# Two weight sums of each Strassen unit move from GpSimd and SBUF to VectorE and PSUM, and some GpSimd operations get a wait on VectorE

## The chip, the cores and the metric

The kernel runs on one core of a Trainium2 chip. The metric is the device time of one execution in microseconds (us). Smaller is better. The engines are called PE (TensorE), DVE (VectorE), ACT (ScalarE), POOL (GpSimd) and SP (SyncE, which only issues transfers here).

## The reference

One decoder layer in float32 on 512 tokens of width 1024: a half-step SwiGLU feed-forward layer (FFN1, inner width 2816), a mixer (sliding-window attention, a causal depthwise convolution of 31 taps, two gates), a second half-step feed-forward layer (FFN2), and a gated embedding. What the change touches are the two feed-forward layers:

```python
def swiglu(h, w_gu, w_down):
    g, u = jnp.split(h @ w_gu, 2, axis=-1)
    return (jax.nn.silu(g) * u) @ w_down
...
        x = x + 0.5 * swiglu(rmsnorm(x, ffn1_norm[i]), ffn1_wgu[i], ffn1_wdown[i])
...
        x = x + 0.5 * swiglu(rmsnorm(x, ffn2_norm[i]), ffn2_wgu[i], ffn2_wdown[i])
```

## The kernel before

**Splitting.** Every float32 product is made of three matmuls in a rounded format: a weight or an activation v is split into hi = round(v), made by ACT, and lo = v - hi, made by DVE (`split_into`, line 701; a few of the lo are "flex", which means that the plan may give them to POOL). `mm3` then adds hi*hi, lo*hi and hi*lo. In the trace these are `whi_wgu`, `wlo_wgu` for the weights of gate and up, and `whi_wd`, `wlo_wd` for the weights of the down product.

**Units.** Most of a feed-forward layer is made of units (`unit`, line 947). A unit multiplies a weight of 2 x 2 blocks, A11, A12, A21, A22, with activations of 2 x 2 blocks by Strassen's way in Winograd's form: seven block products (f = 1 to 7) and some sums in place of eight products. Each of the seven weight forms is split by ACT and DVE, 1024 columns wide (768 in the last units of the down product). Four forms are sums of blocks. Two of them are made by the transfer itself: an accumulating DMA, issued by POOL, adds A22 onto A21, and later another one adds A21 onto A11. The two others are sums made by an engine, in two halves of 512 columns each: form 6 is A21 + A11 (after the first transfer), form 3 is A12 + form 6. They are called `wgu_s` and `wd_s` in the trace. They are flex, lie in SBUF, and POOL makes most of them.

There are 19 units for gate and up (`pair`, line 1062; two blocks of 128 inner columns each) and 12 for the down product (`down`, line 1095). A unit takes four PSUM banks; the running sums b1 and b2 in them are read by DVE and ACT between the products. In `down` DVE adds them onto the residual: operation `x<-wd_a,x` or `x<-wd_b,x`. PE can't go on accumulating in that bank before it is read. After a pair, `act_forms` (line 1046) makes the sums of activations that the down product needs (`f_ta`, `f_tb`, 128x256, flex) and splits them (`f_f`). `sums` (line 917) does the same for the normed input at the start of a layer (`f_xn`, `f_nh`, `f_nl`, `f_t`).

**What sets the order.** The program is recorded first, then a planner (`deadlines`, line 372, and `simulate`, line 404) plays it through with a cost for each operation and takes, on each engine, the ready operation that is due first. The order it finds is written out, and each engine then works through its own list strictly in that order, waiting where data or a buffer are not ready. One line issues everything (L1567), so instructions are told apart by their tiles. The planner knows that a DVE operation and a POOL operation can exclude each other: `op.lock` marks those it takes to be so, and it lets the second wait. Nothing in the emitted program enforces that order. Slots limit how far work runs ahead: 4 raw weight buffers, 4 hi, 4 lo, 8 PSUM banks (line 669). `DOWNS` (line 400) says after which pair the down products of which activations come; `deadlines` gives results in PSUM a due time after their group, 24 for the first plain products (marked `late`).

**The mixer** uses POOL for the convolution of three channel blocks (`y<-y,ct`, one add for each tap, line 1179), for lo splits, and for small work of the attention. At the end of an attention block DVE splits its result into `oT00l` and so on (`values`, line 1360, 128 columns each).

Of the kernel before, what the change touches and what calls it, by code (L numbers as in the profile page):

```python
# [16 lines left out]
P = 128  # L17
# [31 lines left out]
MARGIN = 0.0  # L49

CAPS = {"cz": 2, "ct": 4}
# [176 lines left out]
class Program:  # L228
# [69 lines left out]
    def costs(self, op, eng=None):  # L298
# [19 lines left out]
        elif eng == "DVE":  # L318
# [11 lines left out]
            op.lock = not psum and op.what not in ("tensor_tensor_reduce", "reduce_sum", "tensor_reduce", "reciprocal")  # L330
# [41 lines left out]
def deadlines(prog, when):  # L372
# [26 lines left out]
PLAIN, OWN = (4, 2), (False, False)  # L399
DOWNS = {10: [(0, 4)], 18: [(4, 8)], 20: [(8, 11)]}  # L400
# [3 lines left out]
def simulate(prog, slots):  # L404
# [39 lines left out]
    def can(op, slack):  # L444
# [6 lines left out]
        for v in op.writes:  # L451
            vt = v.vt
            if vt.slot is None:
                need.setdefault(vt.cls, {})[vt] = True
        for c, vts in need.items():
# [13 lines left out]
    def launch(op, t):  # L469
        nonlocal dma_free, aset, lock_dve, lock_pool  # L470
        for v in op.writes:
            vt = v.vt
            if vt.slot is None:
                vt.slot = free[vt.cls].popleft()
                if vt.kind:
                    inuse[vt.kind] += 1
# [195 lines left out]
def record():  # L672
# [274 lines left out]
    def unit(name, src, n, col, forms, own=False, first=None):  # L947
# [12 lines left out]
        sm = {f: [ftile(f"{name}_s{f}_{c}")[:, 0:half] for c in range(2)] for f in (6, 3)}  # L960
        for c in range(2):
            s = slice(c * half, (c + 1) * half)
            nc.flex.tensor_tensor(sm[6][c], A[21][:, s], A[11][:, s], op=ALU.add)
            nc.flex.tensor_tensor(sm[3][c], A[12][:, s], sm[6][c], op=ALU.add)

        def form(f):
            v = sm.get(f) or A[{1: 11, 2: 12, 5: 21, 7: 11, 4: 22}[f]]
            if f in sm and own:
                hi, lo = ([rtile(f"{name}_w{p}{f}_{c}")[:, 0:half] for c in range(2)] for p in "hl")
                for c in range(2):  # L970
                    split_into(hi[c], lo[c], v[c])
                return hi, lo
# [705 lines left out]
```

## Time and profile before

| | |
|---|---|
| median of 3 runs | 1189.03 us (1186.48 to 1191.82) |
| the profiled execution | 1190.71 us, its span 1189.0 us |
| PE, DVE, ACT, POOL busy | 1157.0, 1041.3, 698.0, 582.4 us |
| stages in the span | FFN1 0 to 350, mixer 350 to 800, FFN2 800 to 1150, last gate 1150 to 1189 |
| mean granted TensorE clock | 0.995 |

The span reaches from the first instruction to the last. The profiled execution takes 1.7 us beyond its span. A row of a group in the profile says what is written, what is read, the shape, how often, the busy time, the mean of one in ns, and how long the engine was idle just before such instructions and on whom it waited. Busy times on PE overlap, since matmuls are pipelined; what counts there is the idle time.

### The profile page before, as it was taken

The page shows a single profiled execution, that of the slowest core. Times are in us where ns is not written, and L with a number is a line of the kernel's source. Part 1 is how long each engine was busy: PE and PEld are TensorE (multiplying, and loading weights), DVE is VectorE, ACT ScalarE, POOL GpSimd, SP SyncE. Part 2 cuts the span into 40 slices and gives each one's busy share as a digit, 9 for nine tenths or more (in the row PEclk, how much of TensorE's full clock was granted, in tenths as well). Part 3 has the DMA queues.
Part 4 walks back from the last instruction along what each step waited for, and adds up shares of the span by engine and source line. Part 5 has one row for each costly group of instructions (what it writes and reads, how often), then busy time and mean ns, then how long its engine had stood idle before and what let it go on. Part 6 is the DMA issues. An engine that isn't in the chain of part 4 may idle for free. (4 is left out here: it accounts for less than half of the span.)

```text
span 1189.0 us, 19980 instructions
## 1 busy us (share of the span) xinstructions
PE 1157.0 (97%) x7532; PEld 1056.7 (89%) x7532; DVE 1041.3 (88%) x1582; ACT 698.0 (59%) x1248; POOL 582.4 (49%) x563
## 2 busy tenths in 40 slices
PE   9989999999999999989999999999999999999998
PEld 7889999999999887868788878889999999999986
DVE  6999999978996898999999975579888998798997
ACT  7556546654555679869964472446755456446642
POOL 1666354534425986888799300034663552237400
PEclk9999999999999999999999999999999999999999
DMA  7545657666534321311222323344765566545421
GB/s 242 143 124 143 177 143 170 158 160 158 140 88 123 105 72 43 100 53 37 89 89 93 121 88 95 100 107 109 193 161 160 127 176 156 153 119 139 126 89 71
DMA packets 46752, 146.88 MB, mean 124 GB/s; under 512 B 5696, under 2 KB 10432, under 8 KB 46656
## 3 DMA queue, kind: packets, MB, share of 16 engines
q1 hardware_dynamic: 37584, 114.12, 28.9%
q0 software_dynamic: 8928, 31.46, 15.9%
q8 instruction: 59, 0.97, 0.3%
q14 instruction: 37, 0.30, 0.1%
q10 hardware_dynamic: 144, 0.03, 0.0%
HBM read 143.50 MB, written 2.10 MB: 122 GB/s over the span
## 5 line engine op out<-in xcount | busy, mean ns | idle before, releaser
L1567 DVE TENSOR_TENSOR wlo_wgu<-raw_wgu,whi_wgu 128x1024 fp32r<-128x1024 f32 (+1 forms) x131 | 153.9, 1182 | 20.5 <-ACT whi_wgu L1567 20.2
L1567 ACT ACTIVATE whi_wgu<-raw_wgu 128x1024 fp32r<-128x1024 f32 (+1 forms) x131 | 116.2, 900 | 71.5 <-PE wgu_b L1567 26.4
L1567 PE MATMUL wgu_b<-f_t_h,wlo_wgu 128*128 128x256 f32 x456 | 130.6, 286 | 2.4 <-DVE f_gs L1567 1.8
L1567 PE MATMUL wgu_b<-f_t_l,whi_wgu 128*128 128x256 f32 x456 | 129.9, 285 | 1.5 <-DVE f_t_l L1567 1.5
L1567 PE MATMUL wgu_b<-f_t_h,whi_wgu 128*128 128x256 f32 x456 | 129.7, 284 | 0.0
L1567 POOL TENSOR_TENSOR y<-y,ct 128x509 f32<-128x509 f32 (+28 forms) x90 | 114.1, 1288 | 5.1 <-ACT ct L1567 3.8
L1567 ACT ACTIVATE whi_wd<-raw_wd 128x1024 fp32r<-128x1024 f32 (+1 forms) x60 | 59.3, 988 | 94.2 <-PE wd_b L1567 53.2
L1567 POOL DMA_DIRECT2D raw_wgu<-in_wgu x38 | 34.2, 915 | 162.4 <-DVE x L1567 98.5
L1567 DVE SCALAR_TENSOR_TENSOR cz<-u,dww,cz 128x486 f32<-128x486 f32 (+24 forms) x145 | 101.7, 729 | 1.1
L1567 PEld LDWEIGHTS wgu_b<-f_t_h,wlo_wgu 128*128 128x128 f32 x456 | 87.9, 193 | 3.4 <-ACT f_t_h L1567 2.0
L1567 PEld LDWEIGHTS wgu_b<-f_t_l,whi_wgu 128*128 128x128 f32 x456 | 87.9, 193 | 1.9 <-DVE f_t_l L1567 1.9
L1567 PEld LDWEIGHTS wgu_b<-f_t_h,whi_wgu 128*128 128x128 f32 x456 | 88.0, 193 | 0.0
L1567 PE MATMUL wgu_a<-f_nh,wlo_wgu 128*128 128x256 f32 x304 | 86.2, 284 | 1.1 <-DVE wlo_wgu L1567 1.1
L1567 PE MATMUL wgu_a<-f_nl,whi_wgu 128*128 128x256 f32 x304 | 86.3, 284 | 1.0 <-DVE f_nl L1567 1.0
L1567 PE MATMUL wgu_a<-f_nh,whi_wgu 128*128 128x256 f32 x304 | 86.0, 283 | 0.0
L1567 DVE TENSOR_TENSOR wlo_wd<-raw_wd,whi_wd 128x1024 fp32r<-128x1024 f32 (+1 forms) x60 | 74.2, 1237 | 7.5 <-ACT whi_wd L1567 7.1
L1567 PE MATMUL wd_a<-f_f_h,wlo_wd 128*128 128x256 f32 x264 | 75.3, 285 | 4.4 <-DVE x L1567 4.4
L1567 PE MATMUL wd_b<-f_f_h,wlo_wd 128*128 128x256 f32 x264 | 75.5, 286 | 2.5 <-DVE x L1567 2.0
L1567 PE MATMUL wd_a<-f_f_l,whi_wd 128*128 128x256 f32 x264 | 75.2, 285 | 0.5 <-DVE f_f_l L1567 0.5
L1567 PE MATMUL wd_b<-f_f_l,whi_wd 128*128 128x256 f32 x264 | 75.1, 284 | 0.0
L1567 PE MATMUL wd_b<-f_f_h,whi_wd 128*128 128x256 f32 x264 | 75.1, 284 | 0.0
L1567 PE MATMUL wd_a<-f_f_h,whi_wd 128*128 128x256 f32 x264 | 75.0, 284 | 0.0
(512 smaller groups left out, 4216.9 us busy)
## 6 DMA issues: line engine op xcount, KB each, us to landing
raw_wgu<-in_wgu SPq DMA_DIRECT2D x80, 512.0 KB, 4.4
raw_wgu<-in_wgu POOLq DMA_DIRECT2D x38, 512.0 KB, 5.6
raw_wd<-in_wd SPq DMA_DIRECT2D x32, 512.0 KB, 4.4
raw_wd<-in_wd POOLq DMA_DIRECT2D x16, 512.0 KB, 5.5
raw_wzc<-in_wzc SPq DMA_DIRECT2D x16, 512.0 KB, 3.6
raw_wzg<-in_wzg SPq DMA_DIRECT2D x16, 512.0 KB, 3.6
raw_wd<-in_wd SPq DMA_DIRECT2D x16, 384.0 KB, 3.4
raw_wgu<-in_wgu SPq DMA_DIRECT2D x32, 128.0 KB, 3.8
```

The lines of the kernel that those rows point to most:

```text
L1567: getattr(engines[op.eng], op.what)(*a, **k)
```

## The change

- `unit`: forms 6 and 3 are made by DVE alone (`nc.vector`), into two PSUM tiles, `zs`, one bank each. First z = A21 + A11. When form 6 is due, z is split (ACT reads z, DVE computes lo = z - hi), then z = A12 + z is made in place, and split as form 3. The four SBUF tiles of the sums are gone, and so is the unused option `own`.
- The planner takes both `zs` tiles of a unit together (`mate`), lets only one unit at a time have them (`CAPS`), and not earlier than 24 ahead of their due time (`LEADS`).
- `op.lock` now also holds for DVE operations with one operand in PSUM if two of their inputs lie in SBUF.
- The due time of `late` results is 8 in place of 24.
- `DOWNS`: the first down product follows pair 8 in place of pair 10; the second follows pair 20 in place of pair 18, next to the third.
- `turns` goes through the finished plan. Where the planner started a POOL operation later than its data, its buffer and POOL itself allowed, and a locking DVE operation ended in that time, the POOL operation gets a real wait on that DVE operation. The plan has 46 such waits, 28 of them on POOL's operations in the feed-forward layers.

```diff
-CAPS = {"cz": 2, "ct": 4}
+LATE = 8.0
+LEADS = {"zs": 24.0, "zt": 14.0}
+CAPS = {"cz": 2, "ct": 4, "zs": 2, "zt": 2}
...
-            op.lock = not psum and op.what not in ("tensor_tensor_reduce", "reduce_sum", "tensor_reduce", "reciprocal")
+            two = sum(v.vt.cls != "ps" and v.free() > 1 for v in ins) > 1
+            op.lock = two if psum else op.what not in ("tensor_tensor_reduce", "reduce_sum", "tensor_reduce", "reciprocal")
...
-                            ls = min(ls, gend[o.group] + (24.0 if v.vt.late else 5.0))
+                            ls = min(ls, gend[o.group] + (LATE if v.vt.late else 5.0))
...
-DOWNS = {10: [(0, 4)], 18: [(4, 8)], 20: [(8, 11)]}
+DOWNS = {8: [(0, 4)], 20: [(4, 8), (8, 11)]}
...
         half = n // 2
-        sm = {f: [ftile(f"{name}_s{f}_{c}")[:, 0:half] for c in range(2)] for f in (6, 3)}
-        for c in range(2):
-            s = slice(c * half, (c + 1) * half)
-            nc.flex.tensor_tensor(sm[6][c], A[21][:, s], A[11][:, s], op=ALU.add)
-            nc.flex.tensor_tensor(sm[3][c], A[12][:, s], sm[6][c], op=ALU.add)
+        done = {}
+        cuts = [slice(c * half, (c + 1) * half) for c in range(2)]
+        zs = [nc.tile(f"zs_{name}_{c}", [P, S], F32, "ps")[:, 0:half] for c in range(2)]
+        for z, s in zip(zs, cuts):
+            nc.vector.tensor_tensor(z, A[21][:, s], A[11][:, s], op=ALU.add)
...
+        def summed():
+            done[6], done[3] = pieces(6), pieces(3)
+            for z, s in zip(zs, cuts):
+                split_into(*(p[:, s] for p in done[6]), z)
+                nc.vector.tensor_tensor(z, A[12][:, s], z, op=ALU.add)
+                split_into(*(p[:, s] for p in done[3]), z)
...
+def turns(prog):
+    held, last, vec, free, busy = {}, {}, [], {}, 0.0
...
+        if op.eng == "DVE" and op.lock:
+            vec.append(op)
+        if op.eng == "POOL":
+            if op.lock and op.start > max(ready, busy) + 0.05:
+                for o in reversed(vec[-40:]):
+                    if o.start + o.cost <= op.start + 0.05:
+                        if o.start + o.cost > max(ready, busy):
+                            held[op] = o
+                        break
+            busy = op.start + op.cost
+    return held
...
-            getattr(engines[op.eng], op.what)(*a, **k)
+            made[op] = getattr(engines[op.eng], op.what)(*a, **k)
+            if op in held:
+                tc.add_manual_dep(made[op].ins, made[held[op]].ins.name, sync, reason="port")
```

PE issues the same matmuls as before, and in the mixer in the same order of groups; in the feed-forward layers the down units stand elsewhere. POOL loses 99 sums, DVE had made the other 25 of the 124 and now makes all.

**DVE at the start of FFN1, before.** These rows end the splits of the normed input (`f_nl`), make the activation sums `f_t`, and begin with form 6 of the first unit, whose sum `wgu_s` comes from POOL.

```order
L1567 TENSOR_TENSOR f_nl_640<-f_xn_526,f_nh_541 128x512 [waits DVE_49]
L1567 TENSOR_TENSOR f_nl_646<-f_xn_537,f_nh_551 128x512 [waits DVE_49]
L1567 SCALAR_TENSOR_TENSOR f_t_0_657<-f_t_0_486,f_xn_510 128x256
L1567 SCALAR_TENSOR_TENSOR f_t_0_657<-f_t_0_486,f_xn_517 128x256
L1567 SCALAR_TENSOR_TENSOR f_t_1_674<-f_t_1_504,f_xn_526 128x256
L1567 SCALAR_TENSOR_TENSOR f_t_1_674<-f_t_1_504,f_xn_537 128x256
L1567 TENSOR_TENSOR wlo_wgu_6_696<-wgu_s_0_531,whi_wgu_6_601 128x512 [waits Activation_49]
```

The same place on DVE after the change:

```order
L1611 TENSOR_TENSOR f_nl_653<-f_xn_544,f_nh_561 128x512 [waits Activation_49]
L1611 TENSOR_TENSOR f_nl_660<-f_xn_564,f_nh_580 128x512 [waits Activation_49]
L1611 TENSOR_TENSOR f_gs_669<-f_g_538,f_n_rb 128x512 [waits PE_49]
L1611 TENSOR_TENSOR zs_wgu_0_679<-raw_wgu_21_416,raw_wgu_11_385 128x512 [waits DMASW0_49]
L1611 TENSOR_TENSOR zs_wgu_1_687<-raw_wgu_21_416,raw_wgu_11_385 128x512
L1611 SCALAR_TENSOR_TENSOR f_t_0_696<-f_t_0_487,f_xn_523 128x256
L1611 SCALAR_TENSOR_TENSOR f_t_0_696<-f_t_0_487,f_xn_529 128x256
L1611 SCALAR_TENSOR_TENSOR f_t_1_709<-f_t_1_505,f_xn_544 128x256
L1611 TENSOR_TENSOR wlo_wgu_6_718<-zs_wgu_0_679,whi_wgu_6_698 128x512 [waits Activation_49]
```

The sums now stand in DVE's own list, ahead of `f_t`, and the first of them waits there for the accumulating transfer (`DMASW`).

**POOL in the mixer, before**, around two lists of convolution adds (y_5793 and y_5386 are channel blocks 4 and 2):

```order
L1567 TENSOR_TENSOR y_5793<-y_5793,ct_5_5947 128x507
L1567 TENSOR_TENSOR wlo_wzg_6182<-raw_wzg_5986,whi_wzg_6168 128x1024 [waits DMAHW5_49,PE_49,Activation_49]
L1567 TENSOR_TENSOR y_5793<-y_5793,ct_6_5970 128x506 [waits Pool_49]
L1567 TENSOR_TENSOR y_5386<-y_5386,ct_8_5991 128x504
L1567 TENSOR_TENSOR y_5793<-y_5793,ct_7_6134 128x505 [waits Pool_49]
L1567 TENSOR_TENSOR y_5386<-y_5386,ct_9_6192 128x503 [waits Activation_49,Pool_49]
L1567 TENSOR_TENSOR y_5793<-y_5793,ct_8_6221 128x504 [waits Activation_49,Pool_49]
L1567 TENSOR_TENSOR y_5386<-y_5386,ct_10_6236 128x502 [waits Activation_49,Pool_49]
```

The same place after the change (y_5773 and y_5355):

```order
L1611 TENSOR_TENSOR y_5773<-y_5773,ct_6_5934 128x506
L1611 TENSOR_TENSOR wlo_wzg_6148<-raw_wzg_5960,whi_wzg_6134 128x1024 [waits DMAHW5_49,PE_49,Activation_49]
L1611 TENSOR_TENSOR zq_3_5987<-zq_3_5987,qcs 128x8x16 [waits Pool_49]
L1611 TENSOR_TENSOR y_5355<-y_5355,ct_8_5943 128x504 [waits DVE_49]
L1611 TENSOR_TENSOR zq_3_5987<-zq_3_5987,q_3_w 128x8x16 [waits Pool_49]
L1611 TENSOR_TENSOR y_5773<-y_5773,ct_7_6066 128x505 [waits DVE_49]
L1611 TENSOR_TENSOR y_5355<-y_5355,ct_9_6074 128x503 [waits Pool_49]
L1611 TENSOR_TENSOR y_5773<-y_5773,ct_8_6160 128x504 [waits Activation_49,Pool_49]
```

Two of the adds now wait on DVE. The operations they wait for are `oT00l` and `oT01l` of the last token block, the first of which stands two rows behind the `oT00l` of the block before it in DVE's list.

More of the change, by code (lines that the diff above doesn't have):

```diff
@@ L66, in __init__ @@
         self.late = False
+        self.mate = None
         self.kind = name[:2] if name[:2] in CAPS else None
@@ L462, in can @@
                 return False
+            if slack > min(LEADS.get(vt.kind, 1e9) for vt in vts):
+                return False
             if len(free[c]) < len(vts) + spare:
                 return False
-            if any(vt.kind and inuse[vt.kind] >= CAPS[vt.kind] for vt in vts):
+            if any(vt.kind and inuse[vt.kind] + (vt.mate is not None) >= CAPS[vt.kind] for vt in vts):
                 return False
@@ L471, in launch @@
         for v in op.writes:
[L472 to L476, printed above, removed]
+            for vt in (v.vt, v.vt.mate):
+                if vt is not None and vt.slot is None:
+                    vt.slot = free[vt.cls].popleft()
+                    if vt.kind:
+                        inuse[vt.kind] += 1
         c = op.cost
@@ L945, in record, with unit @@
     lo_, hi_ = slice(0, HS), slice(HS, S)
-    def unit(name, src, n, col, forms, own=False, first=None):
+    def unit(name, src, n, col, forms, first=None):
         A = {}
@@ L988, in times @@
                     c = col(k, m)
-                    wk = part([p[c // half] for p in w], slice(c % half, c % half + P)) if isinstance(w[0], list) else part(w, slice(c, c + P))
+                    wk = part(w, slice(c, c + P))
                     mm3(to[m], wk, x_, start and k == 0, k == len(forms[f]) - 1, skip=f in (3, 4, 6, 7))
@@ L1003, in unit, with ffn @@
             yield 4, m, b1[m], b2[m]
-    def ffn(tag, wgu, wdown, h, gain, ss, after, cuts, wide, plain, own, mid=None):
+    def ffn(tag, wgu, wdown, h, gain, ss, after, cuts, wide, plain, mid=None):
         rb = None
@@ L1538, in record @@
     return nc
+def turns(prog):
+    held, last, vec, free, busy = {}, {}, [], {}, 0.0
+    for vt in prog.tiles:
+        vt.ops = []
+    for op in prog.ops:
+        for vt in op.vts:
+            vt.ops.append(op)
+    for op in sorted(prog.ops, key=lambda o: (o.start, o.i)):
+        ready = max((o.end for o in op.preds), default=0.0)
+        for vt in op.outs:
+            slot = vt.cls, vt.slot
+            was = last.get(slot)
+            if was is not vt:
+                free[slot] = max((o.end for o in was.ops), default=0.0) if was else 0.0
+                last[slot] = vt
+            if vt.ops[0] is op:
+                ready = max(ready, free[slot])
+        if op.eng == "DVE" and op.lock:
[9 more added lines that the diff above has]
+    return held
 def hybrid_layer(tc, aps):
@@ L1562, in real @@
             return v
+        made = {}
+        held = turns(prog)
+        sync = mybir.DependencyInfo(mybir.DependencyClass.Sync, mybir.DependencyReason.DATA)
         for op in sorted(prog.ops, key=lambda o: (o.start, o.i)):
```

35 lines of the change are left out of this document (15 added, 20 removed).

## The prediction

> **What bounds the kernel now.** I read the page first, then busy time by stage, then who waits for whom on PE, then the timeline at the largest waits.
>
> ```profile
> PE 1157.0 (97%) x7532; PEld 1056.7 (89%) x7532; DVE 1041.3 (88%) x1582; ACT 698.0 (59%) x1248; POOL 582.4 (49%) x563
> ```
>
> Busy time by stretches of the span (us, then for PE, weight loads, DVE, ACT and POOL the busy us and the number of instructions, the granted clock, the DMA share and GB/s). The first row is from the middle of FFN1, the others are FFN1, mixer and FFN2:
>
> ```profile
> 200.00:250.00 50.00, 50.00 (x419) 50.00 (x419) 45.99 (x60) 32.12 (x56) 23.99 (x19) 1.00 0.70 177
> ...
> 50.00:350.00 300.00, 291.33 (x2375) 288.72 (x2374) 273.10 (x376) 164.54 (x268) 142.66 (x117) 0.99 0.58 147
> 350.00:800.00 450.00, 440.24 (x2068) 364.55 (x2067) 379.72 (x621) 289.44 (x566) 263.91 (x292) 1.00 0.28 88
> 800.00:1150.00 350.00, 343.48 (x2732) 335.92 (x2731) 318.15 (x455) 202.12 (x331) 157.38 (x127) 1.00 0.55 144
> ```
>
> In the middle of FFN1 PE never stops: nothing can be won there, since the change leaves the matmuls as they are. What can be won is PE's idle time: 8.7 us in FFN1 (300 - 291.33), 9.8 in the mixer, 6.5 in FFN2. In both feed-forward layers DVE is the next fullest engine, with 26.9 and 31.9 us free.
>
> For what did PE wait? The largest entries (total us, times, longest): one from the whole span, then FFN1 (50 to 350), then FFN2 (800 to 1150):
>
> ```profile
> PE sc L1567 <- DVE sga L1567: 4.9, 1, 4.9
> ...
> PE wd_a L1567 <- DVE x L1567: 2.0, 1, 2.0
> PE wgu_b L1567 <- DVE f_gs L1567: 1.8, 1, 1.8
> PE wgu_b L1567 <- DVE f_t_l L1567: 1.5, 2, 1.2
> PE wgu_a L1567 <- DVE wlo_wgu L1567: 1.1, 2, 0.6
> PE wgu_a L1567 <- DVE f_nl L1567: 1.0, 1, 1.0
> ...
> PE wd_a L1567 <- DVE x L1567: 2.4, 2, 1.3
> PE wd_b L1567 <- DVE x L1567: 1.7, 1, 1.7
> PE wgu_a L1567 <- DVE f_t_l L1567: 1.1, 1, 1.1
> ```
>
> Always DVE, in few long pieces: 4.9, 7.4 and 5.2 us. Why was DVE late? The timeline at the largest wait (mixer) and at one in FFN2 (start, us, instruction):
>
> ```profile
> 513.80 7.70 DVE L1567 TENSOR_TENSOR oT00l<-of,oT00h 128x128 fp32r<-128x128 f32 x1
> 512.21 2.40 POOL L1567 TENSOR_TENSOR wlo_wzg<-raw_wzg,whi_wzg 128x1024 fp32r<-128x1024 f32 x1
> 514.57 6.78 POOL L1567 TENSOR_TENSOR y<-y,ct 128x506 f32<-128x506 f32 x6
> 522.75 0.75 PE L1567 MATMUL sc<-kzh,qT_l 128*128 128x512 f32 x1 [4.89 <-DVE sga L1567]
> ...
> 1058.83 3.02 DVE L1567 TENSOR_TENSOR wlo_wd<-wd_s,whi_wd 128x512 fp32r<-128x512 f32 x1
> 1058.91 1.71 POOL L1567 TENSOR_TENSOR f_tb<-f_us,f_us 128x256 f32<-128x256 f32 x2
> ```
>
> A DVE operation of 128 columns lasted 7.70 us: from inside one POOL instruction to the end of six more (514.57 + 6.78 = 521.35). Everything behind it on DVE stood, and PE with it. At 1058.83 it is the same on a smaller scale, and PE's wait of 1.7 us for `x` is the consequence. So an operation of DVE that reads SBUF twice is shut out while POOL works, and a POOL that never pauses shuts it out for its whole run. The Trainium skill ("SBUF — State Buffer", section "Who interferes with whom") says that of two such instructions the later blocks until the earlier instruction ends; by that rule `oT00l` would have gone on at 514.6, PE would have lost nothing here, and the sum below would lack its first term of 6.6 us. The trace disagrees: seven instructions passed.
>
> A long wait costs more than itself. Granted clock (third number from the end) right after the waits of 1.8, 2.0 and 4.9 us:
>
> ```profile
> 75.40:79.20 3.80, 3.61 (x17) 3.64 (x18) 3.80 (x8) 3.40 (x6) 0.71 (x1) 0.55 0.00 0
> 331.40:335.20 3.80, 3.80 (x21) 3.80 (x20) 2.85 (x6) 0.00 (x0) 0.67 (x1) 0.55 0.34 124
> 522.60:526.40 3.80, 3.65 (x11) 2.98 (x12) 3.04 (x11) 2.35 (x5) 0.00 (x0) 0.55 0.00 0
> ```
>
> 0.55 of full speed over 3.8 us loses 1.7 us each time. All in reach: 4.9 + 7.4 + 5.2 + 3 x 1.7 = 22.6 us.
>
> **The change part by part.** DVE's rows by shape (count, busy us, mean ns):
>
> ```profile
> L1567 DVE TENSOR_TENSOR wlo_wgu<-raw_wgu,whi_wgu 128x1024 fp32r<-128x1024 f32 x99 | 141.5, 1430 | 20.1 <-ACT whi_wgu L1567 19.9
> L1567 DVE TENSOR_TENSOR wlo_wgu<-wgu_s,whi_wgu 128x512 fp32r<-128x512 f32 x76 | 69.4, 942 | 0.5 <-ACT whi_wgu L1567 0.5
> L1567 DVE TENSOR_TENSOR wlo_wd<-wd_s,whi_wd 128x512 fp32r<-128x512 f32 x32 | 32.7, 1036 | 0.0
> L1567 DVE TENSOR_TENSOR p_l<-pT,p_h 128x512 fp32r<-128x512 f32 x16 | 10.2, 680 | 0.2
> L1567 DVE TENSOR_TENSOR wlo_wgate<-raw_wgate,whi_wgate 128x1024 fp32r<-128x1024 f32 x8 | 9.6, 1214 | 0.0
> L1567 DVE TENSOR_TENSOR pg_ss_acc<-pg_ss_acc,pg_ss_sq 128x512 f32<-128x512 f32 x5 | 3.5, 692 | 0.0
> L1567 DVE TENSOR_TENSOR pg_ss_acc<-pg_ss_sq,pg_ss_sq 128x512 f32<-128x512 f32 x1 | 0.7, 695 | 0.0
> ```
>
> *Sums added to DVE.* The last two rows are the new operations: two SBUF inputs into PSUM 0.695 us, PSUM plus SBUF in place 0.692. Of 124 sums, 108 have 512 columns: 108 x 0.69 = 74.5 us. The 16 of 384 columns cost between half and all of that; I take three quarters, 0.52: 8.3. DVE made 25 before, at least 25 x 0.69 = 17.3 of its time. Added: 65.5 us. The Trainium skill ("Advanced Engine Details and Errata", section "The Read-Write Bubble") places VectorE nearer to SBUF than to PSUM and advises using it so, which speaks against this move. Rows 692 and 695 against 680 agree in sign, but it is 0.015 us on each of 124, under 2 us of DVE.
>
> *Shut-out time taken off DVE.* `p_l` has the operands that the splits of the sums will have (PSUM and SBUF) and takes 0.680; the same splits from SBUF take 0.942 and 1.036. That is 76 x 0.262 + 32 x 0.356 = 31.3 us. The other splits keep both inputs in SBUF: 99 x (1.430 - 1.214) = 21.4 us shut out, measured against `wlo_wgate`, which runs while POOL is still. They gain as far as POOL has less to do:
>
> ```profile
> L1567 POOL TENSOR_TENSOR wgu_s<-raw_wgu,raw_wgu 128x512 f32<-128x512 f32 x29 | 50.7, 1763 | 39.3 <-DMA raw_wgu<-in_wgu 39.3
> L1567 POOL TENSOR_TENSOR wgu_s<-raw_wgu,wgu_s 128x512 f32<-128x512 f32 x28 | 48.1, 1725 | 11.1 <-DMA raw_wgu<-in_wgu 10.7
> L1567 POOL TENSOR_TENSOR wd_s<-raw_wd,wd_s 128x512 f32<-128x512 f32 x14 | 22.0, 1575 | 12.3 <-DVE f_us L1567 9.8 <-DMA raw_wd<-in_wd 1.8 <-DVE f_f_l L1567 0.7
> L1567 POOL TENSOR_TENSOR wd_s<-raw_wd,raw_wd 128x512 f32<-128x512 f32 x13 | 19.6, 1524 | 38.2 <-DMA raw_wd<-in_wd 31.3 <-DVE f_f_l L1567 6.9
> ```
>
> These alone are 140.4 of POOL's 142.7 + 157.4 = 300.1 us in the two layers, and they come in runs of two to four. With 47% less POOL, some 10 us of the 21.4 go. DVE's balance is then 65.5 - 31.3 - 10 = +24 us in 650, inside its 58.8 free. It stays nearly as full, but it is no longer stopped for several us at a time, and that is what PE felt.
>
> *Waits on PE that go.* In the mixer, the adds behind `wlo_wzg` now wait for `oT00l` and `oT01l`, so POOL pauses there; `oT00l` is held 2.4 us at most in place of 7.7, and PE's 4.9 has no cause left: -4.9 - 1.7 = -6.6 (ends -6.6 and 0). FFN1 loses 7.4 + 2 x 1.7 = 10.8. Two of its waits (`f_nl`, `f_t_l`) are on the crowded list at its start, where the new sums stand ahead of `f_t`; I take two thirds, -7 (ends -10.8 and 0). FFN2: two thirds of 5.2, -3.5 (ends -5.2 and 0), since `f_ta` and `f_tb`, the cause at 1058.9, stay on POOL.
>
> *New waits.* `DOWNS` puts four down units at the end of each layer, so the last pair's activation sums have the (4, 8) units to hide behind; its gain lies in the terms above. Inside a down unit PE needs each `x` operation before it accumulates on, and DVE's list now holds sums that wait for an accumulating transfer. `zs` takes 2 of 8 banks, 4 belong to the running unit, so the next unit starts with 2. For both together I take +2 us (below zero is excluded, as nothing waits less for them; the upper end is the slower rival). The 46 waits on POOL: behind one stand POOL's later operations and the accumulating transfers; POOL is idle for 350 of the 650 us, so zero. `LATE` and `LEADS` only shift due times: zero.
>
> Sum: -6.6 - 7 - 3.5 + 2 = -15.1. The profiled execution would take 1190.7 - 15.1 = 1175.6; it lies 1.7 above the median, so the median 1189.0 becomes 1173.9, say 1174.
>
> **The rivals.**
>
> *DVE keeps PE waiting all the same (0.20).* DVE stays at over 90% in both layers, and operations that come in order fall late without POOL's help. Then only the mixer's wait goes, and half of the rest comes back in new places with its clock: 1189 - 6.6 + 2 = 1184, between 1180 and 1189. For it: +24 us. Against it: in the rows 200 to 250 DVE was 46.0 of 50 with PE never waiting.
>
> *DVE stands at the transfers (0.13, slower).* POOL waited for accumulating transfers before it summed:
>
> ```profile
> POOL wgu_s L1567 <- DMA raw_wgu<-in_wgu: 49.9, 14, 6.9
> POOL wd_s L1567 <- DMA raw_wd<-in_wd: 40.0, 10, 7.2
> ```
>
> 24 waits, 89.9 us, 3.7 each. Now the sum stands in DVE's list and everything behind it waits too, the `x` operations above all. DVE has 58.8 - 24 = 35 us left to hide that. Beyond 35 it reaches PE, and from 35 + 15 = 50 us on the kernel is slower. With two thirds inherited (60 us): 1174 + 25 = 1199; with all, 1229. For it: the lists are strict, and the wait is in the order. Against it: POOL came early because it was free half the time, and the planner places a DVE sum by its due time.
>
> *The change doesn't do what it says (0.07).* POOL's waits don't open a gap where DVE needs it, or the runs of `f_ta`, `f_tb` and `y` shut DVE out in other places: 1189, give or take 5.
>
> **How the numbers follow.** The forecast case, 1165 to 1182, has 0.60. A difference under 0.5% (6 us) can't be told from none here, since the three runs spread over 5.3 us. Faster by more: 0.60, and half of the first rival: 0.70. Slower by more: 0.13 and a little of the last one, less what of the transfers' rival ends near zero: 0.12. Within: 0.18. The range starts where everything in reach goes (1189.0 - 22.6 = 1166, less 1 for the spread), 1165, and ends at 1191, which takes in the first rival and most of the last and leaves the transfers' rival out.
>
> **What would show it.** Right: no `oT` operation over 2.7 us on DVE; `wlo_wgu<-zs` at 0.68 and `zs` sums at 0.69 to 0.9 us; POOL busy near 160 us in the two layers; PE's waits under 8 us in all, and fewer drops of the clock. Wrong: entries of DVE waiting on `raw_wgu` or `raw_wd` transfers that sum to more than 35 us; PE's idle time in the layers at 15 us or more; a wait of PE for banks held by `zs`.

## The result, and the profile after

The changed kernel takes 1171.38 us (1170.37 to 1172.17, 4 runs), the kernel before 1190.42 in the same comparison: ratio 0.9844, 95% interval 0.9816 to 0.9872. It is faster by 19 us. The prediction said 1174 in a range from 1165 to 1191, so the number was right. The experiments show which parts of the working behind it hold.

Two corrections to the sections ahead of the prediction. No tile's `mate` is ever set, so the two `zs` tiles aren't taken as one; only `CAPS` holds them to two at a time. And FFN2 starts before 800: its first matmul stands at 782.0 in the kernel before and at 763.8 after the change.

The span is 1169.1 us. The page's busy times, to be held against PE 1157.0, DVE 1041.3 and POOL 582.4 of before:

```profile
PE 1152.4 (99%) x7532; PEld 1054.3 (90%) x7532; DVE 997.4 (85%) x1670; ACT 692.2 (59%) x1246; POOL 440.9 (38%) x475
```

Busy time in the stretches of the prediction (PE, weight loads, DVE, ACT, POOL, the granted clock). The last one ends at 1130, because FFN2 ends earlier:

```profile
50.00:350.00 300.00, 297.19 (x2453) 296.22 (x2452) 267.72 (x434) 167.50 (x274) 72.66 (x69) 0.99 0.61 152
350.00:800.00 450.00, 444.79 (x2090) 367.88 (x2090) 378.49 (x634) 293.59 (x579) 272.27 (x300) 1.00 0.29 89
800.00:1130.00 330.00, 327.71 (x2632) 321.67 (x2631) 284.25 (x472) 187.72 (x310) 78.54 (x77) 1.00 0.59 148
```

PE's idle time in them was 8.7, 9.8 and 6.5 us; now it is 2.8, 5.2 and 2.3. That is 14.7 us less. But the second stretch now holds the start of FFN2. Between the first and the last matmul of each stage PE idled 9.0, 9.8 and 6.2 us before, and idles 2.8, 2.6 and 3.9 now, 15.5 us less in all. Stretches of 1.9 us in which the clock was under 0.75 were six before, and there is one now; summed as (1 - clock) x 1.9 that is 4.8 us before and 1.0 after, another 3.8. Together that is roughly 19 of the span's 19.9 us. Whom PE waited for (total, times, longest; the wait for `ones` at the start of the program left out):

```profile
PE wgu_b L1611 <- DVE f_gs L1611: 3.3, 2, 1.8
PE gb L1611 <- DVE s L1611: 1.2, 1, 1.2
...
PE wgu_b L1611 <- ACT f_gs L1611: 1.1, 1, 1.1
```

The waits for `sc` (4.9) and for the `x` operations are gone, and no piece is longer than 1.8 us. DVE by shape (count, busy, mean ns, idle before):

```profile
L1611 DVE TENSOR_TENSOR wlo_wgu<-raw_wgu,whi_wgu 128x1024 fp32r<-128x1024 f32 x99 | 124.7, 1261 | 37.6 <-ACT whi_wgu L1611 37.5
L1611 DVE TENSOR_TENSOR wlo_wgu<-zs_wgu,whi_wgu 128x512 fp32r<-128x512 f32 x76 | 49.1, 679 | 4.9 <-ACT whi_wgu L1611 4.8
L1611 DVE TENSOR_TENSOR zs_wgu<-raw_wgu,zs_wgu 128x512 f32<-128x512 f32 x38 | 25.7, 684 | 0.0
L1611 DVE TENSOR_TENSOR zs_wgu<-raw_wgu,raw_wgu 128x512 f32<-128x512 f32 x38 | 25.2, 703 | 0.6 <-DMA raw_wgu<-in_wgu 0.6
```

The single prices of the prediction are here: the splits at 679 ns in place of 942, the sums at 684 to 703. The other splits fell further than expected, to 1261 ns from 1430: 16.7 of their 21.4 us went, where 10 were taken. And the slower rival is dead: 60 us or more of waits on accumulating transfers were to pass to DVE, and DVE waited 0.6 us for one. In this plan the sums stand far enough behind their transfers.

At the largest wait of before, the mixer's, POOL's timeline (start, us, instruction, idle time and its releaser):

```profile
500.57 2.42 POOL L1611 TENSOR_TENSOR wlo_wzg<-raw_wzg,whi_wzg 128x1024 fp32r<-128x1024 f32 x1
502.93 0.54 POOL L1611 TENSOR_TENSOR zq<-zq,qcs 128x128 f32<-128x128 f32 x1
503.69 1.36 POOL L1611 TENSOR_TENSOR y<-y,ct 128x504 f32<-128x504 f32 x1 [0.23 <-DVE oT00l L1611]
```

and DVE's:

```profile
502.37 0.77 DVE L1611 TENSOR_TENSOR oT00l<-of,oT00h 128x128 fp32r<-128x128 f32 x1
```

POOL waits 0.23 us for `oT00l`, and `oT00l` takes 0.77 us in place of 7.70.

### The profile page after: what moved, and what is told of

Same layout as the page of the kernel before. It is cut to its first block, busy times and chain, and to the rows that moved or that the text cites. A ratio compares the mean times of both kernels' runs of the same rounds, so it can differ in the third digit from the quotient of the medians.

```text
span 1169.1 us, 19917 instructions
## 1 busy us (share of the span) xinstructions
PE 1152.4 (99%) x7532; PEld 1054.3 (90%) x7532; DVE 997.4 (85%) x1670; ACT 692.2 (59%) x1246; POOL 440.9 (38%) x475
## 4 chain that ended last, share of the span: by engine, by line
PE 88%; DVE 7%; ACT 3%; issue 1%; DMA 1%; POOL 0%; DVEq 0%; POOLq 0%; ACTq 0%
PE wgu_b L1611 17%; PE wgu_a L1611 12%; PE wd_b L1611 10%; PE wd_a L1611 8%; PE cp L1611 4%; PE gb L1611 4%; PE ap L1611 4%; PE wo L1611 4%; PE pg L1611 3%; PE cb L1611 3%; PE ca L1611 3%; PE ga L1611 3%; PE f_g L1611 2%; PE f_u L1611 2%; PE q0b L1611 2%; PE q1b L1611 2%
## 5 line engine op out<-in xcount | busy, mean ns | idle before, releaser
L1611 DVE TENSOR_TENSOR wlo_wgu<-raw_wgu,whi_wgu 128x1024 fp32r<-128x1024 f32 (+1 forms) x131 | 137.3, 1056 | 38.1 <-ACT whi_wgu L1611 37.9
L1611 POOL TENSOR_TENSOR y<-y,ct 128x511 f32<-128x511 f32 (+27 forms) x90 | 110.4, 1244 | 4.5 <-DVE oT12l L1611 1.5
L1611 DVE SCALAR_TENSOR_TENSOR cz<-u,dww,cz 128x504 f32<-128x504 f32 (+24 forms) x145 | 100.6, 730 | 0.8
L1611 DVE TENSOR_TENSOR wlo_wd<-raw_wd,whi_wd 128x1024 fp32r<-128x1024 f32 (+1 forms) x60 | 69.4, 1158 | 8.5 <-ACT whi_wd L1611 8.0
```

The lines of the kernel that those rows point to most:

```text
L1611: made[op] = getattr(engines[op.eng], op.what)(*a, **k)
```

## The experiments

The change has three parts that can be taken apart: the sums on DVE (S), the planner's other numbers `LATE` and `DOWNS`, which give another order (O), and the waits of `turns` (W). W follows from the plan, so the number of waits differs. All ratios are to the kernel before, run on the same chip.

| kernel | sums | order | waits | us | ratio | 95% interval |
|---|---|---|---|---|---|---|
| the change | DVE | new | 46 | 1171.38 | 0.9844 | 0.9816 to 0.9872 |
| `e1_no_waits` | DVE | new | 0 | 1185.84 | 0.9949 | 0.9926 to 0.9972 |
| `e2_only_waits` | POOL | old | 73 | 1172.83 | 0.9876 | 0.9833 to 0.9919 |
| `e3_only_plan` | POOL | new | 0 | 1205.87 | 1.0151 | 1.0111 to 1.0190 |
| `e4_one_wait` | POOL | old | 1 | 1181.64 | 0.9932 | 0.9909 to 0.9955 |
| `e5_waits_ffn` | POOL | old | 62 | 1176.80 | 0.9903 | 0.9860 to 0.9946 |
| `e6_new_sums_old_plan` | DVE | old | 45 | 1186.67 | 0.9993 | 0.9960 to 1.0025 |
| `e7_old_sums_new_plan` | POOL | new | 70 | 1184.16 | 0.9964 | 0.9933 to 0.9995 |
| `e8_sums_in_sbuf` | DVE, in SBUF | new | 53 | 1175.32 | 0.9890 | 0.9861 to 0.9920 |
| `e9_more_waits` | DVE | new | 93 | 1178.95 | 0.9923 | 0.9895 to 0.9952 |
| `e10_e6_plus_one` | DVE | old | 46 | 1181.96 | 0.9940 | 0.9923 to 0.9957 |
| `e11_old_plan_more` | POOL | old | 148 | 1176.60 | 0.9901 | 0.9872 to 0.9929 |

The same by stage, from the first matmul of a stage to its last, in us. PE has the same number of matmuls in each stage in all of these kernels. The figures are those of the one profiled execution of each, and the last two columns are PE's idle time:

| kernel | FFN1 | mixer | FFN2 | idle in the layers | idle in the mixer |
|---|---|---|---|---|---|
| the kernel before | 353.2 | 423.7 | 356.6 | 15.1 | 9.8 |
| the change | 343.9 | 414.9 | 353.9 | 6.8 | 2.6 |
| `e1_no_waits` | 346.6 | 426.4 | 354.3 | 9.1 | 10.7 |
| `e2_only_waits` | 348.6 | 416.7 | 350.6 | 6.8 | 4.5 |
| `e3_only_plan` | 355.8 | 426.6 | 363.8 | 20.9 | 15.3 |
| `e4_one_wait` | 350.9 | 416.5 | 357.1 | 13.7 | 4.2 |
| `e5_waits_ffn` | 348.5 | 422.4 | 350.6 | 6.9 | 8.8 |
| `e6_new_sums_old_plan` | 345.3 | 426.1 | 357.8 | 12.0 | 14.1 |
| `e7_old_sums_new_plan` | 352.9 | 417.4 | 357.4 | 13.9 | 7.8 |
| `e9_more_waits` | 345.4 | 421.4 | 353.7 | 7.4 | 6.7 |
| `e10_e6_plus_one` | 344.7 | 421.4 | 357.6 | 11.8 | 8.9 |

My theory after the result was the prediction's: the sums' move takes POOL out of DVE's way in the feed-forward layers, and a wait or two mends the mixer. The rival: the waits carry the gain wherever the sums are made.

### The change without its waits

```diff
-        held = turns(prog)
+        held = {}
```

> The changed kernel without its 46 waits, all else and every engine's order the same. Theory (GpSimd shuts VectorE out; the sums gave about 12 us, the waits about 7 in the mixer): the run of convolution adds behind wlo_wzg shuts oT00l out again, PE waits 4 to 5 us at sc and the clock drops once; 1171 + 6 = 1177 (1174 to 1180). Rival A (only the place of the sums counts): 1171, oT00l short as it is with the waits. Rival B (the waits carry the gain): 1185 or more.

1185.84 us: the number of rival B. PE's largest waits, then the timeline of DVE at two of them:

```profile
PE wgu_b L1611 <- DVE f_gs L1611: 6.2, 2, 4.1
PE kvb L1611 <- DVE mix_h_l L1611: 4.1, 2, 2.3
PE o L1611 <- DVE of L1611: 3.9, 1, 3.9
```

```profile
352.42 5.61 DVE L1611 SCALAR_TENSOR_TENSOR mix_h_l<-x,g_all,mix_h_h 128x512 fp32r<-128x512 f32 x2
...
501.83 6.09 DVE L1611 TENSOR_TENSOR wlo_wzg<-raw_wzg,whi_wzg 128x1024 fp32r<-128x1024 f32 x1
```

Two splits in a row took 5.61 us, each shut out by one POOL instruction of 2.8, and one split took 6.09 because POOL ran on without a pause; PE waited 2.3 and 3.9 us for what stood behind them.

To measure shut-out time as a whole I summed, over all DVE instructions of the two feed-forward layers, the duration less the shortest of the same operation and shape in the same trace: about 124 us before, 38 with the change, and 40 here. So two thirds of it goes without any wait.

By stage, the two layers take 700.9 us here, 8.9 less than before, of the 12.0 that the change takes off them. The mixer takes 426.4, which is 2.7 more than before and 11.5 more than with the change. So in the layers the theory holds and the new sums and order give most of the gain; in the mixer the waits give more than the 7 us that I gave them, because more than one operation is held up there without them.

### The waits alone

The kernel before, with the function `turns` and its waits, and nothing else:

```diff
+        made = {}
+        held = turns(prog)
...
-            getattr(engines[op.eng], op.what)(*a, **k)
+            made[op] = getattr(engines[op.eng], op.what)(*a, **k)
+            if op in held:
+                tc.add_manual_dep(made[op].ins, made[held[op]].ins.name, sync, reason="port")
```

> The kernel before, in its own order, with the waits that the same rule finds in its plan (sums still on GpSimd in SBUF; none of the waits falls on the convolution adds at oT00l of the third token block). Theory: some long runs in the feed-forward layers are broken, the sums come later, the mixer's wait of 4.9 us stays: 1187 (1183 to 1191). Rival A (only the place of the sums counts): 1190. Rival B (the waits carry the gain): 1175 or less.

1172.83 us: rival B, 14 us below the theory. Shut-out time in the two layers is about 117 us, nearly as before, and POOL is as busy as before (in the first stretch 140.86 us against 142.66):

```profile
50.00:350.00 300.00, 294.59 (x2413) 292.86 (x2412) 276.16 (x384) 167.11 (x271) 140.86 (x119) 0.99 0.58 149
...
800.00:1120.00 320.00, 318.75 (x2604) 315.83 (x2604) 289.28 (x416) 187.42 (x308) 151.87 (x122) 1.00 0.57 150
```

Yet PE stands still only 1.25 us in the second row, and its waits for DVE are short:

```profile
PE wgu_b L1601 <- DVE wlo_wgu L1601: 2.3, 2, 1.3
PE wd_a L1601 <- DVE x L1601: 1.7, 2, 1.2
```

The waits take little off DVE's shut-out time. They move POOL's instruction behind the DVE operation that the plan put first, and PE idles 6.8 us in the two layers in place of 15.1. So the sum of shut-outs isn't what the kernel pays for; what remains of them falls where PE isn't waiting. The two layers take 699.2 us, 10.6 less than before.

The mixer takes 7.0 us less too, since PE's wait of 4.9 us for `sc` is gone. None of the waits accounts for that at its place. DVE and POOL issue the same rows there in the same order as before, and `oT00l` starts 0.79 us ahead of the end of `wlo_wzg` (before: 0.81); but this time it is let in at that end, though the adds follow without a pause as before:

```profile
509.50 0.93 DVE L1601 TENSOR_TENSOR oT00l<-of,oT00h 128x128 fp32r<-128x128 f32 x1
510.24 7.07 POOL L1601 TENSOR_TENSOR y<-y,ct 128x506 f32<-128x506 f32 x6
```

So these 7 us can't be put down to the waits with certainty.

### The new order alone

```diff
-                            ls = min(ls, gend[o.group] + (24.0 if v.vt.late else 5.0))
+                            ls = min(ls, gend[o.group] + (8.0 if v.vt.late else 5.0))
...
-DOWNS = {10: [(0, 4)], 18: [(4, 8)], 20: [(8, 11)]}
+DOWNS = {8: [(0, 4)], 20: [(4, 8), (8, 11)]}
```

> The kernel before with the other places of the down products and the earlier due time of the first results (8 in place of 24), sums and waits as before. Theory: the down units hide the last pair's sums, at most the waits at the ends of the two layers go (2.0 + 1.3 us and one drop of the clock, 1.7), and GpSimd's runs shut VectorE out as before: 1188 (1184 to 1193). Rival (the new order carries the gain): 1175 or less.

1205.87 us, slower than before, where both theories had it equal or faster. PE's waits, and DVE's timeline at the longest:

```profile
PE wgu_b L1567 <- DVE wlo_wgu L1567: 8.0, 3, 4.5
PE o L1567 <- DVE of L1567: 8.0, 1, 8.0
PE wgu_b L1567 <- DVE f_t_l L1567: 4.3, 3, 2.8
```

```profile
509.62 10.09 DVE L1567 TENSOR_TENSOR wlo_wzg<-raw_wzg,whi_wzg 128x1024 fp32r<-128x1024 f32 x1
```

A split of 1.2 us was shut out for 8.9 us, through a run of some fifteen POOL instructions. The clock adds to the bill (two of three stretches, PE busy first, clock third from the end):

```profile
62.30:71.80 9.50, 6.05 (x27) 5.60 (x27) 9.50 (x9) 0.75 (x2) 4.77 (x6) 0.50 0.82 240
518.30:525.90 7.60, 3.56 (x9) 2.83 (x10) 7.48 (x13) 1.93 (x6) 0.33 (x1) 0.55 0.23 71
```

Summed as above, the slow stretches of this kernel make 11.6 us, against 4.8 before. So the new numbers are not a gain of their own: alone they cost 15 us by the medians and 18 by the ratio.

### One wait in the mixer

The kernel before, in which the first add behind `wlo_wzg` waits for `oT00l`:

```diff
+        held = {reading("y4", "ct4_6"): reading("oT00l", "of0_2")}
```

> The kernel before with one wait more: the first convolution add behind wlo_wzg waits for the oT00l of the third token block. Theory: GpSimd pauses, oT00l lasts under 1.5 us in place of 7.7, PE's wait of 4.9 us at sc and the clock drop behind it go, and nothing else changes: 1190.4 - 6.6 = 1183.8 (1182 to 1186). Rival (the wait at sc had another cause, or comes back elsewhere): 1190.

1181.64 us, a little under the range of the theory: one wait on POOL is worth 0.7%, and the mixer takes 7.2 us less. PE's wait for `sc` is gone from the list, and the operation that lasted 7.70 us lasts 0.96:

```profile
511.46 0.96 DVE L1573 TENSOR_TENSOR oT00l<-of,oT00h 128x128 fp32r<-128x128 f32 x1
```

### The feed-forward layers' waits

As in the second experiment, but only for POOL's operations in the two layers (62 waits, 39 of them on the sums):

```diff
+        held = {o: d for o, d in turns(prog).items() if o.outs[0].name[:3] in ("f1_", "f2_", "wgu", "wd1", "wd2")}
```

> The kernel before, in its own order, with only those of its 73 waits that fall on operations of the feed-forward layers (62); the 11 in the mixer left out. New theory (the waits carry the gain, wherever the sums are made: 18 us on the old order, of which some 8 in the mixer as the run with one wait showed): 1191 - 10 = 1181 (1178 to 1184). Rival (the one large wait in the mixer and its clock drop are nearly all; the rest of the 18 came from shifts): 1189, or 1183 if the large wait is missed by a shift in time.

1176.80 us (interval of the ratio 0.9860 to 0.9946, so between 6 and 17 us of gain), a little more gain than expected. In the profiled execution (1178.87 us) the mixer's wait stands as it was:

```profile
PE sc L1601 <- DVE sga L1601: 4.9, 1, 4.9
```

By stage the two layers take 10.7 us less than before. So the waits give about as much in the feed-forward layers (1.0%) as the one wait gives in the mixer (0.7%); all together gave 1.2%.

The ten times of this kernel fall into two groups, five from 1170.5 to 1174.7 us and five from 1178.9 to 1183.3. With the pair of traces above, one with the hold of `oT00l` and one without it, this suggests that the hold comes in some executions of the same lists and not in others. That isn't shown: there is one trace for each kernel.

### The new sums in the old order

The change with `LATE` and `DOWNS` as before:

```diff
-LATE = 8.0
+LATE = 24.0
...
-DOWNS = {8: [(0, 4)], 20: [(4, 8), (8, 11)]}
+DOWNS = {10: [(0, 4)], 18: [(4, 8)], 20: [(8, 11)]}
```

> The changed kernel with the down products and the due time of the first results as before (10, 18, 20; 24 in place of 8): new sums, 45 waits. New theory (waits carry the gain; sums in PSUM and plan each add 1 to 5 us): 1174 (1170 to 1179). Rival (the new sums need the new places of the down products, since the last pair's work and VectorE's sums crowd the ends of the layers): 1181 or more.

1186.67 us, the rival's number, but mostly for another reason:

```profile
PE ap L1611 <- DVE wlo_wap L1611: 10.2, 1, 10.2
PE wgu_b L1611 <- DVE f_gs L1611: 6.2, 1, 6.2
```

The first is a shut-out of 8.49 us, through a run of POOL that follows without a pause; the rule of `turns` finds no gap here and sets no wait (DVE, then POOL):

```profile
629.00 8.49 DVE L1611 TENSOR_TENSOR ln_acc<-ln_acc,y 128x512 f32<-128x512 f32 x1
```

```profile
628.84 1.29 POOL L1611 TENSOR_TENSOR ln_acc<-y,y 128x512 f32<-128x512 f32 x1
630.09 1.03 POOL L1611 TENSOR_TENSOR y<-y,ct 128x482 f32<-128x482 f32 x1
631.09 2.33 POOL L1611 TENSOR_TENSOR wlo_wzg<-raw_wzg,whi_wzg 128x1024 fp32r<-128x1024 f32 x1
633.38 1.25 POOL L1611 TENSOR_TENSOR ln_acc<-ln_acc,y 128x512 f32<-128x512 f32 x1
634.60 2.33 POOL L1611 TENSOR_TENSOR wlo_wap<-raw_wap,whi_wap 128x1024 fp32r<-128x1024 f32 x1
```

The second, 6.2 us at the start of FFN2, has no shut-out in it: by the old due time an operation `f_gs<-f_g`, for whose PSUM bank PE waits, stands late in DVE's list, behind a new sum, at 808.0. In the change none of PE's waits over 0.25 us ends with such an operation. That points to `LATE`, which would then have a use, and only with the new sums; it wasn't undone by itself. By stage, 11.2 us of the loss against the change lie in the mixer and 5.3 in the layers.

### The old sums in the new order, with waits

```diff
-                            ls = min(ls, gend[o.group] + (24.0 if v.vt.late else 5.0))
+                            ls = min(ls, gend[o.group] + (8.0 if v.vt.late else 5.0))
...
-DOWNS = {10: [(0, 4)], 18: [(4, 8)], 20: [(8, 11)]}
+DOWNS = {8: [(0, 4)], 20: [(4, 8), (8, 11)]}
...
+        held = turns(prog)
```

> The kernel before with the new places of the down products and the new due time, and the 70 waits that the rule finds there: old sums on GpSimd. Without waits this order took 1205.9. New theory (waits remove what GpSimd's runs cost, which was most in this order): 1177 (1172 to 1182), so the waits give 25 us or more here. Rival (the order itself is bad for the old sums): 1190 or more.

1184.16 us, between the two. The waits take 1.9% or 22 us off what this order took without them. What is left against the change, 1.2%, is the move of the sums, with the waits that go with its plan. PE's largest wait is a new one, for ACT:

```profile
PE wgu_b L1601 <- ACT whi_wgu L1601: 6.9, 2, 4.2
```

Its longer piece, 4.2 us, ends at 61.3 with the split of a sum that POOL had finished only at 60.6; POOL had itself waited 3.65 us for DVE before an earlier sum. So a wait on POOL isn't free where PE needs POOL's result next.

### The sums on DVE, in SBUF

```diff
-        zs = [nc.tile(f"zs_{name}_{c}", [P, S], F32, "ps")[:, 0:half] for c in range(2)]
+        zs = [nc.tile(f"zs_{name}_{c}", [P, S], F32, "a")[:, 0:half] for c in range(2)]
```

> The changed kernel with its sums on VectorE but in SBUF in place of PSUM, planned anew, 53 waits. New theory (with the waits in place it matters little whether the splits of the sums can be shut out; GpSimd has little to do in these layers): 1173 (1170 to 1178). Rival (PSUM is what frees VectorE: 31 us of shut-out time come back on splits that read SBUF twice): 1180 or more.

1175.32 us, as the theory had it. Shut-out time in the layers is about 41 us, against 38 with PSUM. In this order it matters that the sums leave POOL; PSUM adds some 4 to 6 us, and since the two intervals overlap, even that isn't clear of the noise.

### A wider rule for the waits

In place of the rule of the change: each POOL operation that the plan starts after a locking DVE operation, and that is the first such since it, waits for it.

```diff
+        if op.eng == "POOL" and op.lock and last is not None:
+            if last.start + last.cost <= op.start + 0.05:
+                held[op] = last
+            last = None
```

> The changed kernel with 93 waits of GpSimd on VectorE in place of 46: every delayed GpSimd operation on SBUF that the planner put behind a VectorE operation on SBUF (and not on top of it) now waits for that one, not only where the plan left a gap ahead of it. Theory (single long shut-outs of operations that TensorE waits for are what costs, and a wait ends them): the longest ones left in the changed kernel's trace, 4.07 us at 638.1, 2.93 at 645.9 and the 2.66 and 2.35 at 343 to 348, go or halve, and the time is 1168 (1165 to 1171). Rival (the 46 waits have taken what there was; more of them only make GpSimd late in the mixer, where it is busy 272 of 450 us): 1174 or more, with TensorE waiting for GpSimd's wlo_wzg.

1178.95 us, slower than the change by 0.8% or some 9 us. The text above is wrong in one thing: the wider rule doesn't contain the other. It keeps 29 of the 46 waits, adds 64 and drops 17, among them those that held POOL's two `wlo_wzc` behind `mix_h_l` at the start of the mixer. DVE there (first the change, then this kernel):

```profile
349.73 1.40 DVE L1611 SCALAR_TENSOR_TENSOR mix_h_l<-x,g_all,mix_h_h 128x512 fp32r<-128x512 f32 x2
```

```profile
351.38 5.61 DVE L1593 SCALAR_TENSOR_TENSOR mix_h_l<-x,g_all,mix_h_h 128x512 fp32r<-128x512 f32 x2
```

PE's largest waits in this kernel:

```profile
PE wgu_b L1593 <- DVE f_gs L1593: 4.0, 2, 2.5
PE kvb L1593 <- DVE mix_h_l L1593: 3.4, 2, 2.3
```

The wait of `kvb` is back as it was in the kernel with no waits at all. By stage the mixer takes 421.4 us in place of 414.9. That wait and a drop of the clock right behind it (0.50 from 354.9 to 360.6) are most of the difference. So the likeliest cause is that the waits which count were dropped; a kernel with both sets was not tried. Of the 64 new waits 50 are on operations outside the two layers.

### The one wait that the sixth kernel lacked

```diff
+        held[reading("y4", "ct4_30")] = reading("ln_acc1", "y6")
```

> The kernel with the new sums and the old due times (1186.67 us), plus one wait: GpSimd's add of the last tap (it reads ct4_30) waits for VectorE's sum of the layer norm that reads y6, which was shut out for 8.49 us at 629.0 through five GpSimd instructions while TensorE waited 10.2 us in one piece for what follows it. Theory (that one shut-out, and the clock's drop of some 1.7 us behind it, is most of what this kernel lacks): 1175 to 1177, and TensorE's wait of 10.2 is gone. Rival (the wait only moves the blockage to the next GpSimd run, or VectorE's list is late here anyway): 1184 or more.

1181.96 us, between the two. The operation of 8.49 us takes 1.69, but the run behind it goes on, and the next two DVE operations in the chain now meet it:

```profile
628.56 1.69 DVE L1615 TENSOR_TENSOR ln_acc<-ln_acc,y 128x512 f32<-128x512 f32 x1
...
632.03 2.81 DVE L1615 TENSOR_TENSOR wlo_wap<-raw_wap,whi_wap 128x1024 fp32r<-128x1024 f32 x1
...
636.61 2.77 DVE L1615 TENSOR_TENSOR wlo_wap<-raw_wap,whi_wap 128x1024 fp32r<-128x1024 f32 x1
```

PE's wait for `wlo_wap` goes from 10.2 to 5.0. One wait mends half of it, and the mixer takes 4.7 us less; more of them at this place were not tried.

### The kernel before with the wider rule

The rule above on the kernel before's own plan, which gives 148 waits.

> The kernel before with its own order and sums on GpSimd, and 148 waits of the wider rule in place of the 73 with which it took 1172.83 us; 46 of them sit on the sums. Theory (long single shut-outs cost): 1170 (1167 to 1173), within a few us of the changed kernel with 93 waits, so that moving the sums is worth little once GpSimd waits its turn everywhere. Rival (the sums' place matters: GpSimd with 440 us of its own plus the sums falls behind when it waits at every operation): 1177 or more, with TensorE waiting for wlo_wgu.

1176.60 us, between the two (interval of the ratio 0.9872 to 0.9929). Neither of the two kernels with the wider rule beats the change, and no other kernel here does.

### The lock by itself

Not the layer: pieces in which GpSimd makes a run of 512-column adds in SBUF and VectorE starts one operation beside it. The names say the length of the run; `chain` makes each add of the run wait for the one before, in `turn` the third of eight was to wait for VectorE, `pd` writes to PSUM, `pa` lies in PSUM.

> Not the layer: only VectorE and GpSimd work, and the output is not the layer's. In each piece GpSimd starts a run of 1, 2, 4 or 8 adds of 128x512 in SBUF (1.03 to 1.24 us each in the traces), and VectorE starts one add some 0.55 us into the run. Theory (the lock is kept through a whole run of instructions that follow one another without a pause): VectorE's add of two SBUF tiles takes 0.68 with no run, and about 1.3, 2.5, 4.9 and 9.7 us; the same 4.9 where it writes PSUM; 0.68 to 0.70 where one input is in PSUM; with GpSimd's third add waiting for it, 2.5 of a run of 8. In a chain in which each GpSimd add waits for the one before, less, if the pause between them lets VectorE in. Rival (one instruction at most is waited for): 1.3 us for every length. The reverse, one GpSimd add started in a run of six VectorE adds: by the theory some 4.5 us, by the rival under 2.

```profile
L76 DVE TENSOR_TENSOR pd_ss_p<-a,b 128x512 f32<-128x512 f32 x2 | 2.8, 1382 | 0.0
L76 DVE TENSOR_TENSOR d_eightp<-a,b 128x512 f32<-128x512 f32 x1 | 1.8, 1771 | 0.0
...
L76 DVE TENSOR_TENSOR d_chainp<-a,b 128x512 f32<-128x512 f32 x1 | 1.8, 1750 | 0.0
...
L78 DVE TENSOR_TENSOR pd_ps_p<-pa,b 128x512 f32<-128x512 f32 x2 | 1.4, 690 | 0.0
L76 DVE TENSOR_TENSOR d_onep<-a,b 128x512 f32<-128x512 f32 x1 | 1.4, 1373 | 0.0
...
L76 DVE TENSOR_TENSOR d_turnp<-a,b 128x512 f32<-128x512 f32 x1 | 0.7, 683 | 0.0
...
L76 DVE TENSOR_TENSOR d_nonep<-a,b 128x512 f32<-128x512 f32 x1 | 0.7, 680 | 0.0
```

VectorE ran ahead of GpSimd, so some operations fell into the run ahead of their own: `d_eight` starts in the third add of the run of four (17.93), `d_chain` in the sixth of the run of eight (26.93), and `d_turn` in the chain (33.47). So a run whose third add waits for VectorE was not tried. The rest holds, and my theory falls: in the middle of a run of four or eight, VectorE waits for one instruction (1.75 to 1.77 us, of which 0.68 its own), as in a run of one (1.37). The next instruction of the run then waits for VectorE and takes 1.71 us in place of 1.26. In the chain it goes in at once (0.68), 0.1 us before the end of an add. With two inputs from SBUF and the output in PSUM it is shut out all the same (1.38); with one input in PSUM it isn't (0.69). The reverse, one GpSimd add beside six of VectorE, also waits for one only:

```profile
69.83 1.64 POOL L104 TENSOR_TENSOR y_revp<-x,b 128x512 f32<-128x512 f32 x1 [0.81 <-DVE x L100]
```

## Why the prediction was right, and where it was not

- **What can be won is PE's idle time and the clock behind it: right.** Roughly 15.5 + 3.8 of the span's 19.9 us came from there, of the 22.6 named as in reach.
- **The prices of single operations: right.** 0.679 against 0.680 for the splits of the sums; the sums at 0.684 to 0.703 against 0.69.
- **DVE's balance, +24 us in the two layers: wrong in sign.** DVE's busy time there, from first to last matmul, fell from 639.7 to 606.6 us. The sums added 63 us, near the 65.5 of the prediction, but shut-out time fell by 86 and not by 41. The prediction counted only the splits of the sums and of `raw_wgu`; the splits `f_f_l` of activations, for instance, were held up for 24 us in all, and now for 5. Its conclusion, that DVE is no longer stopped for long, stands all the more.
- **"Waits on PE that go", the mixer: the place was right, the size too small.** -6.6 was predicted, put down to one wait, and that wait alone gives 8 us (interval 5 to 11). With the change the mixer takes 8.8 us less. Without its waits the new plan loses 2.7 there, through other holds (`mix_h_l`, `wlo_wzg`), so the waits are worth 11.5 us in it.
- **"Waits on PE that go", FFN1 and FFN2, -7 and -3.5: the size was right, the cause not the only one.** The two layers took 709.8 us before and take 697.8 now, 12.0 less. The gain was to come from DVE being held up less by POOL's sums, and without any wait the new sums and the new order do give 8.9 of it. But with POOL's sums left where they were, the waits of these layers alone give 10.7, while shut-out time hardly falls. PE's idle time in the layers, 15.1 us before, ends at 9.1 by the first way, 6.9 by the second and 6.8 with both.
- **"The 46 waits on POOL: [...] so zero": the step that failed.** I asked only what a wait costs POOL, and not what it does for DVE beyond one place in the mixer. On three settings of the rest the waits, the mixer's among them, are worth 1.2% (old sums, old order), 1.9% (old sums, new order) and 1.05% (new sums, new order): 15, 22 and 12 us. In the first, some 7 us of the trace are the hold of `oT00l` that went without a wait at its place. In the change itself the traces give 11.5 us in the mixer, where 6.6 were booked, and 3.1 in the layers, where none were.
- **"`LATE` and `LEADS` only shift due times: zero": wrong for `LATE` together with `DOWNS`, whose effect the prediction put into other terms.** Together these two cost 15 to 18 us with the old sums and no waits; with the new sums the old values cost 15 to 18 us. By stage, 11.2 of these lie in the mixer, where the one long run at 629 makes PE wait 10.2 us; the one wait added there brought back 4.7. These parts don't add up, since each new order lays POOL's runs against other DVE operations. `LEADS` was not tried by itself.
- **"New waits", +2: about right.** PE waits for banks of `wgu_b` until `f_gs` has read them: 1.5 us for DVE at 794.4 and 1.1 for ACT at 824.0, both in FFN2, where the kernel before has no such wait. With the sums in SBUF, which take no bank, the longest is 0.5 (in a plan of its own). No wait for `x` is left, and DVE waited 0.6 us for a transfer.
- **The trace against the rule: half right.** The Trainium skill ("SBUF — State Buffer", section "Who interferes with whom") has the later instruction block until the earlier one ends. The probe agrees in all pieces, 1.37 to 1.77 us; the rows 7.70, 8.49, 6.09 and 10.09 of the layer don't. The conclusion in the prediction, that a POOL which never pauses shuts DVE out for its whole run, is too strong: such holds are rare.
- **What would show it.** Held: no `oT` operation over 2.7 us (the longest is 2.57), the prices, fewer drops of the clock, and POOL's busy time, which fell by 148 us in the two layers where 140 were expected. Not quite: PE's waits for DVE between 50 and 1150 us sum to 9.0 us and not under 8, from 23.0 before.

That the sum came out near is in part luck. In the layers with no waits, the sums' move gives 18.7 us in the new order (719.6 to 700.9) and the new order by itself costs 9.8 (709.8 to 719.6); the prediction had neither figure, and its 10.5 lies near their difference.

What the sums' move is worth remains tied to the order: 24 us with the new order and no waits, 14 with the new order and waits, and a loss of 14 with the old order and waits (the kernel in which the rule left one long run without a wait; 8 with the one wait added). Whether the change beats the kernel with the waits alone isn't settled: 0.9844 and 0.9876, from different comparisons, have intervals that overlap.

## What to carry to other kernels

Where two engines exclude each other, what counts is not how long the one is held up in all, but whether the hold falls on an operation that the bound engine is about to need; look for the single long ones in the timeline. A semaphore wait that makes the less urgent engine keep the planned order can be cheap while that engine is half idle: here a single one was worth 0.7% and the 62 in the feed-forward layers 1.0%, against 1.6% for the whole change. Price a wait by both sides: what stands behind the engine that waits, and what the other one is spared. And cut stages by their own first and last work, not by fixed times, when two kernels are compared.

## What the runs showed of the hardware

- **When the lock passes on.** Over the traces of the kernel before, the change and the eleven kernels of the layer I looked at each DVE operation held up by over 0.3 us, at the end of a POOL instruction that another follows closely (from 0.1 us of overlap to 0.3 of pause). At more than 800 such places DVE came in at that first end, at 20 it didn't, and it then stayed out for one to fourteen more instructions. The 20 are a few places again and again, among them `oT00l` behind `q_rs`, a split behind `q_v<-q_sq`, `ln_acc` behind a copy of one column, and `wlo_wzc` behind a tap of 487 columns. What sets them apart is open: at `oT00l` the same rows with nearly the same offsets gave 7.70 us in one trace and 0.93 in another, and the probe, in which VectorE came in each time, doesn't reproduce it.
- **Some small POOL operations overlap in the trace.** Of 56 pairs of `f_ta` and `f_tb` (256 columns) that follow one another closely in the kernel before, 9 overlap by 0.3 us or more, the others by about 0.04 or not at all. At each of the 9 DVE was being held up. At 1058.8 a split of 3.02 us was held through three: the two in the prediction's row of 1.71 us, and a third that starts at 1060.31, before their end at 1060.62.
- **A write to PSUM doesn't free an operation from the lock.** What counts is two inputs from SBUF: 1.38 us against 0.69 in the probe. The Trainium skill ("SBUF — State Buffer", section "Who interferes with whom") states it by inputs too, and these rows agree. In the change's trace `mix_ss_acc`, which reads two SBUF tiles and writes PSUM, took 2.35 us at 347.5:

```profile
347.47 2.35 DVE L1611 TENSOR_TENSOR mix_ss_acc<-mix_ss_sq,mix_ss_sq 128x512 f32<-128x512 f32 x1
```
